# A two-block transformer kernel: softmax off GpSimd, convolutions ahead of the state-space heads, decay rows spread by transfers

## The chip, the cores and the metric

The kernel runs on one core of one Trainium2 chip. The metric is the device time of the whole program in microseconds; lower is better. The program takes 512 tokens of 1024 numbers in float32 through two blocks, once.

## The reference, cut to what matters

The first block is a mixer layer (windowed means, a sparse attention over selected keys), a cross attention to 256 memory tokens and a SwiGLU layer. The second block is two hybrid layers, and each of them runs a sliding-window attention and a state-space ("SSD") scan on the same input:

```python
def hybrid_layer(x, ...):
    q, k, v, z_attn, z_ssm, xbc, dt_raw = split(x @ w_in)
    attn = sliding_window_attention(q, k, v, sinks) * silu(z_attn)
    xbc = silu(causal_depthwise_conv(xbc, conv_w, conv_b))      # 12 x 128 channels
    xs, bm, cm = split(xbc)                                     # 8 + 2 + 2
    y = ssd_chunked(xs, softplus(dt_raw + dt_bias), -exp(a_log), bm, cm) + xs * d_skip
    ssm = gated_rmsnorm(y, z_ssm, ssm_norm_w)                   # y * silu(z), two groups
    return layer_norm(ALPHA * x + concat(attn, ssm) @ w_out, ln_g, ln_b)

def ssd_chunked(xs, dt, a, bm, cm):                             # 4 chunks of 128, 16 heads of 64
    a_cs = cumsum(dt * a) in each chunk
    y_diag[l] = sum_s (cm[l] . bm[s]) * exp(a_cs[l] - a_cs[s]) * xdt[s]    # s <= l
    y_off[l]  = (cm[l] . state before the chunk) * exp(a_cs[l])
    return y_diag + y_off
```

## The kernel before, in words

All activations stand with 128 channels on the partitions and 512 tokens along the row. Each float32 operand of a matmul is split into a rounded part and a rest (`hi`, `lo`), and a product is three matmuls: `hi*hi` and `hi*lo` (L147, L148), then `lo*hi` (L152). A projection of 1024 channels onto 128 is 24 matmuls (`proj`, `mm3`). `weights()` brings one such 128x1024 piece: SP issues the load of `wraw` (L104), ScalarE casts it to `whi` (L107), VectorE subtracts for `wlo` (L108); each has three buffers. `split` and `pair` do the same to activations (L129, L130, or L132, L133 with a scale).

A hybrid layer (`hybrid`) goes in this order: the first four gates z and dt; the convolutions of B, C and of channels 0 to 4 (`conv`: a projection, L905 on ScalarE, three passes on VectorE, a tanh); then a loop of eight head pairs. Each turn holds one more projection (channels 5 to 7, then the last four gates), `decay(j+1)` for the next pair and `heads(j)` for this one. Then the two keys (L132, L133 and copies of each half to the other half of the partitions, L1114 on GpSimd), the token values (96 matmuls, L1127 to L1129), and the attention loop over 16 heads (`scores`, `transposed`, `values`) with its own projections of queries and gates.

`decay(j)` makes, for both heads of a pair, the 128x512 factors `exp(-(relu(a_s - a_l))) * cb`. A matmul with a column of `sel` spreads a head's row of `a_cs` over the partitions in PSUM (L1041), ScalarE takes the difference and relu in four pieces (L1045), exponentials of the row (L1047) and of the whole (L1048), and GpSimd or VectorE multiplies by `cb` (L1049). `heads(j)` has 16 matmuls L1061 and 6 of L1067, and VectorE adds up (L1069 to L1071); L1098 is the gate, and L1078 the norm's scaling. The softmax of the attention is normalised at L1169, half on GpSimd and half on VectorE, ahead of the transposes L1183; L1154 and L1155 are the scores. The memory attention does the same at L763.

The feed-forward stage keeps `x` in DRAM (`xd`): 16 writes at L788 and 16 reads at L868, on ScalarE's queue.

SP's instructions stand in program order. On the other engines a scheduler sets the order when the program is built; each engine then goes through its list strictly in order, and a row whose input is late holds all rows behind it.

## Time and profile before

| | |
|---|---|
| median of 3 runs | 1673.09 us (1672.94 to 1673.29) |
| the profiled execution | 1672.5 us, span 1670.7 us |
| mean granted TensorE clock | 0.993 |
| TensorE matmul busy | 1621.6 us (97%) |
| VectorE, ScalarE, GpSimd busy | 1115.1 us (67%), 838.0 us (50%), 239.2 us (14%) |
| DMA | 166.50 MB, 100 GB/s over the span |
| the two hybrid layers | about 834 to 1657 us of the span |

The profile is of one execution. The engines' rows give busy time; the chain follows the end of the program back to what released each step; the waits list what ended each idle time of an engine. Where TensorE is idle, nothing else makes up for it unless the chain shows otherwise.

### The profile page before, as it was taken

What the parts mean: (1) busy time and instruction counts of PE and PEld (TensorE: products, weight loads), DVE (VectorE), ACT (ScalarE), POOL (GpSimd) and SP (SyncE); (2) the same over time, 40 slices, a digit from 0 to 9 for tenths busy, and PEclk for the clock granted to TensorE, in tenths of its full rate; (3) what the DMA queues carried; (4) which work ended last, traced back from release to release, by engine and by line L of the source; (5) the groups of instructions that cost most, each with busy time, mean ns of one, the idle gap of its engine ahead of it and who ended that gap; (6) DMA issues with size and microseconds to landing.
All of it is one profiled execution on the core that took longest, in us unless ns stands there. A gap on an engine that the chain in (4) does not pass through costs nothing.

```text
span 1670.7 us, 24187 instructions
## 1 busy us (share of the span) xinstructions
PE 1621.6 (97%) x9046; PEld 1362.4 (82%) x9046; DVE 1115.1 (67%) x2199; ACT 838.0 (50%) x1648; POOL 239.2 (14%) x267
## 2 busy tenths in 40 slices
PE   8999999999999999999999999999999999999996
PEld 5778888889888888889988677777998867777786
DVE  6779866548885545523677888765487788866447
ACT  4443255336763233223554776664355477766424
POOL 2010113010200000000000223221230023222121
PEclk9999999999999999999999999999999999999998
DMA  6522322143143233234632122111452211212133
GB/s 223 196 96 76 119 96 76 64 151 119 62 150 104 89 101 101 87 102 129 212 93 89 38 64 89 64 64 56 141 177 82 79 38 57 96 61 65 66 103 112
DMA packets 57719, 166.50 MB, mean 100 GB/s; under 512 B 6673, under 2 KB 15841, under 8 KB 57601
## 3 DMA queue, kind: packets, MB, share of 16 engines
q1 hardware_dynamic: 49216, 155.21, 29.0%
q10 hardware_dynamic: 8384, 9.73, 1.8%
q8 instruction: 71, 1.16, 0.3%
q14 instruction: 48, 0.39, 0.1%
HBM read 158.61 MB, written 8.93 MB: 100 GB/s over the span
## 4 chain that ended last, share of the span: by engine, by line
PE 78%; DVE 11%; ACT 5%; issue 2%; POOL 2%; DMA 1%; SPq 0%; ACTq 0%; DVEq 0%; POOLq 0%
PE psmm L148 21%; PE psmm L152 21%; PE psmm L147 21%; DVE wlo L108 2%; POOL w L1169 2%; PE psmm L175 2%; PE psmm L173 2%; PE psmm L174 2%; ACT w L1164 1%; DVE w L1160 1%; DVE G L130 1%; PE pstr L1061 1%; PE pstr L1183 1%; PE pslg L561 1%; PE pslg L1020 1%
## 5 line engine op out<-in xcount | busy, mean ns | idle before, releaser
L147 PE MATMUL psmm<-G,whi 128*128 128x512 f32 (+1 forms) x1196 | 468.5, 393 | 1.3 <-ACT whi L107 1.3
L148 PE MATMUL psmm<-G,whi 128*128 128x512 f32 (+1 forms) x1196 | 464.3, 389 | 0.0
L108 DVE TENSOR_TENSOR wlo<-wraw,whi 128x1024 fp32r<-128x1024 f32 (+3 forms) x265 | 320.4, 1210 | 184.8 <-ACT whi L107 99.2
L107 ACT CAST whi<-wraw 128x1024 fp32r<-128x1024 f32 (+3 forms) x265 | 270.9, 1025 | 340.3 <-PE psmm L148 291.3
L152 PE MATMUL psmm<-G,wlo 128*128 128x512 f32 (+1 forms) x1196 | 296.3, 388 | 0.0
L148 PEld LDWEIGHTS psmm<-G,whi 128*128 128x128 f32 x1196 | 225.3, 188 | 47.2 <-issue 4.2
L147 PEld LDWEIGHTS psmm<-G,whi 128*128 128x128 f32 x1196 | 225.3, 188 | 47.2 <-issue 2.4
L152 PEld LDWEIGHTS psmm<-G,wlo 128*128 128x128 f32 x1196 | 222.7, 189 | 46.4 <-issue 1.5
L148 PE MATMUL psmm<-R,whi 128*128 128x256 f32 (+1 forms) x732 | 222.7, 326 | 0.0
L147 PE MATMUL psmm<-R,whi 128*128 128x256 f32 (+1 forms) x732 | 222.6, 326 | 0.0
L147 PEld LDWEIGHTS psmm<-R,whi 128*128 128x128 f32 x732 | 139.2, 190 | 11.8 <-issue 0.3
L148 PEld LDWEIGHTS psmm<-R,whi 128*128 128x128 f32 x732 | 139.2, 190 | 11.5
L152 PE MATMUL psmm<-R,wlo 128*128 128x256 f32 (+1 forms) x732 | 138.1, 326 | 0.0
L152 PEld LDWEIGHTS psmm<-R,wlo 128*128 128x128 f32 x732 | 112.8, 190 | 11.5
L198 POOL TENSOR_TENSOR acc<-acc,sq 128x512 f32<-128x512 f32 (+1 forms) x42 | 53.4, 1272 | 454.4 <-ACT sq L197 454.4
L1164 ACT ACTIVATE w<-w,st 128x256 f32<-128x256 f32 (+1 forms) x128 | 60.2, 471 | 33.5 <-DVE st L1162 33.2
L1169 POOL TENSOR_SCALAR w<-w,st 128x256 f32<-128x256 f32 x64 | 46.1, 730 | 134.6 <-DVE st L1167 127.0
L209 ACT ACTIVATE sq<-ht 128x512 f32<-128x512 f32 (+1 forms) x48 | 29.4, 613 | 58.5 <-DVE ht L907 29.3
L1049 POOL TENSOR_TENSOR R<-R,R 128x512 f32<-128x512 f32 x16 | 21.7, 1353 | 228.3 <-ACT R L1048 228.3
L907 DVE SCALAR_TENSOR_TENSOR ht<-psmm,cwh,ht 128x511 f32<-128x511 f32 (+2 forms) x72 | 53.5, 743 | 1.2
L837 DVE TENSOR_TENSOR sq<-psmm,G 128x512 f32<-128x512 f32 (+1 forms) x24 | 15.5, 645 | 57.3 <-PE psmm L152 57.3
L566 POOL TENSOR_TENSOR G<-G,G 128x384 f32<-128x384 f32 (+2 forms) x24 | 28.9, 1217 | 162.1 <-DMA G<-ts 93.4
(348 smaller groups left out, 2701.8 us busy)
## 6 DMA issues: line engine op xcount, KB each, us to landing
wraw<-w_in SPq DMA_DIRECT2D x112, 512.0 KB, 3.4
wraw<-w_out SPq DMA_DIRECT2D x56, 512.0 KB, 3.8
wraw<-w_down SPq DMA_DIRECT2D x24, 512.0 KB, 3.5
wraw<-w_gate SPq DMA_DIRECT2D x22, 512.0 KB, 3.3
wraw<-w_up SPq DMA_DIRECT2D x22, 512.0 KB, 3.3
wraw<-w_down SPq DMA_DIRECT2D x12, 384.0 KB, 3.2
wraw<-w_proj_attn SPq DMA_DIRECT2D x8, 512.0 KB, 3.4
ts<-t SPq DMA_DIRECT2D x4, 640.0 KB, 7.0
```

What stands on the lines that cost most here:

```text
L107: nc.scalar.copy(hi[:, :n], raw[:, :n])
L108: nc.vector.tensor_tensor(lo[:, :n], raw[:, :n], hi[:, :n].bitcast(F32), ALU.subtract)
L147: nc.tensor.matmul(out, whi[:, c], xh, start=start and k == 0, stop=False)
L148: nc.tensor.matmul(out, whi[:, c], xl, start=False, stop=False)
L152: nc.tensor.matmul(out, wlo[:, c], xh, start=False, stop=stop and k == n - 1)
L173: nc.tensor.matmul(o, whi[:, cc], xh[:, c], start=k == 0 and i % 2 == 0, stop=False, skip_group_check=True)
L174: nc.tensor.matmul(o, whi[:, cc], xl[:, c], start=False, stop=False, skip_group_check=True)
L175: nc.tensor.matmul(o, wlo[:, cc], xh[:, c], start=False, stop=k == n - 1, skip_group_check=True)
L198: (eng or nc.gpsimd).tensor_tensor(acc, acc, t, ALU.add)
L907: nc.vector.scalar_tensor_tensor(y[:, s:], pt[:, : S - s], cw(3 - s), y[:, s:], ALU.mult, ALU.add)
L1164: nc.scalar.activation(prs[b], prs[b], AF.Exp, bias=nm[:, b : b + 1], accum_out=sm[:, b : b + 1])
L1169: (nc.gpsimd if b % 2 else nc.vector).tensor_scalar(prs[b], prs[b], rc[:, b : b + 1], 1.0, ALU.mult, ALU.mult)
```

## The change

It does seven things. Weights' rests are cut in pieces of 512 columns inside the attention loop only. The memory softmax and the attention softmax are normalised on VectorE alone. The 32 `xd` transfers go from ScalarE's queue to SP's. The last three `w_o_mem` pieces are held in buffers of their own, and three feed-forward weights are loaded ahead. The rows `a_cs` and their exponentials are written to DRAM once per layer, and four SP transfers per head pair spread them over the partitions, two pairs ahead; the 16 matmuls per layer of L1041 and the exponentials of L1047 go, half of the relu passes go to VectorE (L1057) and the product with `cb` is all VectorE's (L1059). Convolutions 5 and 6 come before the heads; the loop's turns then hold convolution 7, four gates, the token values and the two keys. The keys' half copies, eight per layer, are SP transfers (L1101).

```diff
--- before.py
+++ after.py
@@ -75,6 +75,7 @@
...
+        self.piece = 2 * S
...
@@ -105,7 +106,9 @@
         hi = self.wp.tile([P, 1024], F32R, tag="whi", bufs=3, name=self.nm("whi"))
         lo = self.wp.tile([P, 1024], F32R, tag="wlo", bufs=3, name=self.nm("wlo"))
         nc.scalar.copy(hi[:, :n], raw[:, :n])
-        nc.vector.tensor_tensor(lo[:, :n], raw[:, :n], hi[:, :n].bitcast(F32), ALU.subtract)
+        for o in range(0, n, self.piece):
+            c = slice(o, min(o + self.piece, n))
+            nc.vector.tensor_tensor(lo[:, c], raw[:, c], hi[:, c].bitcast(F32), ALU.subtract)
         return hi, lo
 
     def held(self, src, tag, n=1024):
@@ -760,7 +763,7 @@
                 nc.scalar.activation(p, bank[:, 256 * i : 256 * i + 256], AF.Exp, bias=nm[:, i : i + 1], scale=r[:, i : i + 1], accum_out=sm[:, i : i + 1])
             nc.vector.reciprocal(rc, sm)
             for i, p in enumerate(parts):
-                (nc.vector if i else nc.gpsimd).tensor_scalar(p, p, rc[:, i : i + 1], 1.0, ALU.mult, ALU.mult)
+                nc.vector.tensor_scalar(p, p, rc[:, i : i + 1], 1.0, ALU.mult, ALU.mult)
             return parts
 
         def values(hd, c, prs):
@@ -785,7 +788,7 @@
 
         def each(k, c, x):
             scale(k, c, x)
-            nc.scalar.dma_start(self.xd[k][:, c], x)
+            nc.sync.dma_start(self.xd[k][:, c], x)
 
         def out(j, c):
             o = self.ps()[:, :256]
@@ -800,13 +803,12 @@
             nc.sync.dma_start(kv[i].bitcast(F32), self.spill[i])
         wo = [self.held(a["w_o_mem"][0], "G")]
         queries(B, lambda k: values(k // 2, A, pa[k // 2]) if k % 2 else None)
-        wo += [self.weights(a["w_o_mem"][1]), self.weights(a["w_o_mem"][2])]
+        wo += [self.held(a["w_o_mem"][j], "R") for j in (1, 2, 3)]
         for j in range(8):
-            if j == 4:
-                wo.append(self.weights(a["w_o_mem"][3]))
             out(j, A)
             if j < 4:
                 pb.append(logits(j, B))
+        self.ahead = [self.weights(z) for z in (a["w_gate"][0], a["w_up"][0], a["w_gate"][1])]
         for j in range(4):
             values(j, B, pb[j])
             if j == 0:
@@ -842,8 +844,7 @@
         full = slice(0, S)
         hid += self.pairs("R", 2)
         g = [self.f("ht") for _ in range(2)]
-        first = [self.weights(z) for z in (a["w_gate"][0], a["w_up"][0], a["w_gate"][1])]
-        first.append(self.held(a["w_up"][1], "R"))
+        first = self.ahead + [self.held(a["w_up"][1], "R")]
         for c in self.HALVES:
             for i, pt in enumerate(self.units_by_k(first, h, c)):
                 (up if i % 2 else gate)(i // 2, c, g[i // 2][:, c], pt)
@@ -865,7 +866,7 @@
 
         def src(k, c):
             t = self.s("w256", (P, 256), 9)
-            nc.scalar.dma_start(t, self.xd[k][:, c])
+            nc.sync.dma_start(t, self.xd[k][:, c])
             return t
 
         self.h = self.pairs("G")
@@ -880,9 +881,6 @@
         self.dist = self.load("dist", [P, 256], nc.sync)
         self.sinks = self.load("sinks", [P, 32], nc.sync)
         self.small = self.load("small16", [16, 4], nc.sync)
-        sel = self.load("sel", [48, 16], nc.sync)
-        self.sel = self.cp.tile([48, 16], F32R, tag="selr", name="selr")
-        nc.vector.tensor_copy(self.sel, sel)
 
     def hybrid(self, L):
         nc, a = self.nc, self.a
@@ -952,9 +950,10 @@
         nc.vector.tensor_scalar(av, av, -1.0, None, ALU.mult)
         nc.vector.tensor_scalar(e, dtf, av, None, ALU.mult)
         nc.vector.tensor_tensor_scan(acs, seg, e, 0.0, ALU.mult, ALU.add)
-        ahl = self.s("ahl", (48, S), dt=F32R)
-        nc.vector.memset(ahl.bitcast(F32), 0.0)
-        self.split(acs, ahl[0:16, :], ahl[32:48, :])
+        self.acsd = self.dp.tile([2, 16, S], F32, tag=f"acs{L}", name=f"acs{L}")
+        nc.scalar.dma_start(self.acsd[0], acs)
+        nc.scalar.activation(seg, acs, AF.Exp)
+        nc.scalar.dma_start(self.acsd[1], seg)
         B, C = BC[:2], BC[2:]
 
         ptd = self.ps("tr")
@@ -1030,24 +1029,34 @@
             xs.append(conv(j, "G"))
         xs.append(conv(4, "G"))
         tokens(0)
+        for j in range(5, 7):
+            xs.append(conv(j, "G"))
+
+        def decay_rows(j):
+
+            dfs, ee = [self.f("R") for _ in range(2)], self.f("R")
+            for e_, df in enumerate(dfs):
+                row = self.acsd[:, 2 * j + e_, :]
+                nc.sync.dma_start(df, row[:1].broadcast_to([P, S]))
+                nc.sync.dma_start(ee[64 * e_ : 64 * e_ + 64, P:], row[1:, P:].broadcast_to([64, S - P]))
+            return dfs, ee
 
         def decay(j):
 
-            ee = self.f("R")
-            dfs = []
-            for e_ in range(2):
+            dfs, ee = rows.pop(0)
+            if j < 6:
+                rows.append(decay_rows(j + 2))
+            for e_, df in enumerate(dfs):
                 hd = 2 * j + e_
-                pb = self.ps("lg")
-                nc.tensor.matmul(pb, self.sel[:, hd : hd + 1].broadcast_to([48, P]), ahl, start=True, stop=True)
-                df = self.f("R")
                 for c in range(4):
                     cc = slice(c * P, (c + 1) * P)
-                    nc.scalar.activation(df[:, cc], pb[:, cc], AF.Relu, bias=atok[:, c * 16 + hd : c * 16 + hd + 1], scale=-1.0)
-                rows = slice(64 * e_, 64 * e_ + 64)
-                nc.scalar.activation(ee[rows, P:], pb[rows, P:], AF.Exp)
-                nc.scalar.activation(df, df, AF.Exp, scale=-1.0)
-                (nc.vector if e_ else nc.gpsimd).tensor_tensor(df, df, cb[hd // 8], ALU.mult)
-                dfs.append(df)
+                    at = atok[:, c * 16 + hd : c * 16 + hd + 1]
+                    if e_:
+                        nc.scalar.activation(df[:, cc], df[:, cc], AF.Relu, bias=at, scale=-1.0)
+                    else:
+                        nc.vector.tensor_scalar(df[:, cc], df[:, cc], at, 0.0, ALU.subtract, ALU.min)
+                nc.scalar.activation(df, df, AF.Exp, scale=-1.0 if e_ else 1.0)
+                nc.vector.tensor_tensor(df, df, cb[hd // 8], ALU.mult)
             return dfs, ee
 
         def heads(j, ws, ee):
@@ -1079,16 +1088,54 @@
                 cat[8 + i] = self.pair(t, "R")
 
 
+
+        top, bot = slice(0, 64), slice(64, P)
+        kt = []
+
+        def keys(j):
+            pt = self.proj(W[j], h)
+            ks = [[self.r("G") for _ in range(2)] for _ in range(2)]
+            for (kh, kl), r, o in zip(ks, (top, bot), (bot, top)):
+                self.split(pt[r], kh[r], kl[r], 0.125)
+                for t in (kh, kl):
+                    nc.sync.dma_start(t[o].bitcast(F32), t[r].bitcast(F32))
+            return ks
+
+        def token_values():
+            vs = [self.f("G") for _ in range(2)]
+            pv = [self.ps("mm") for _ in range(2)]
...
+            for v, pt in zip(vs, pv):
+                nc.scalar.copy(v, pt)
+            return vs
+
+
         cat = [None] * 16
         accs = []
+        rows = [decay_rows(0), decay_rows(1)]
         ws = decay(0)
         for j in range(8):
             g = j // 4
-            if j < 3:
-                xs.append(conv(5 + j, "G"))
-            elif j < 7:
+            if j == 0:
+                xs.append(conv(7, "G"))
+            elif j < 5:
                 zs.append(self.f("R"))
-                silu(zs[-1], self.proj(W[25 + j], h))
+                silu(zs[-1], self.proj(W[27 + j], h))
+            elif j == 5:
+                vs = token_values()
+            else:
+                kt.append(keys(j - 6))
             nxt = decay(j + 1) if j < 7 else None
             if j == 3:
                 tokens(1)
@@ -1101,35 +1148,6 @@
             if j % 4 == 0:
                 accs.append(self.f("acc"))
             self.sumsq(y, accs[-1], j % 4 == 0)
-
-
-        top, bot = slice(0, 64), slice(64, P)
-        kt = []
-        for j in range(2):
-            pt = self.proj(W[j], h)
-            ks = [[self.r("G") for _ in range(2)] for _ in range(2)]
-            for (kh, kl), r, o in zip(ks, (top, bot), (bot, top)):
-                self.split(pt[r], kh[r], kl[r], 0.125)
-                for t in (kh, kl):
-                    nc.gpsimd.tensor_copy(t[o], t[r].bitcast(F32))
-            kt.append(ks)
...
         gated_norm(1, accs[1])
 
         def scores(t, q):
@@ -1166,7 +1184,7 @@
             nc.vector.tensor_tensor(sm, sm, es, ALU.add)
             nc.vector.reciprocal(rc, sm)
             for b in range(4):
-                (nc.gpsimd if b % 2 else nc.vector).tensor_scalar(prs[b], prs[b], rc[:, b : b + 1], 1.0, ALU.mult, ALU.mult)
+                nc.vector.tensor_scalar(prs[b], prs[b], rc[:, b : b + 1], 1.0, ALU.mult, ALU.mult)
             return prs
 
         def transposed(prs):
@@ -1207,6 +1225,7 @@
             return qs
 
 
+        self.piece = S
         q = queries(0)
         gate, pts = {}, {}
         prs = None
@@ -1231,6 +1250,7 @@
                 cat[i] = self.pair(gate[i], "R", 0.5)
             prs = nxt
 
+        self.piece = 2 * S
         order = list(range(8, 16)) + list(range(8))
         acc, acc2, rs = self.f("acc"), self.f("acc"), self.f("rs")
         vs = [self.f("G") for _ in range(KD)]
```

The lists that the scheduler makes of it move. In each layer the new lines have these numbers: L147, L148, L152 are L150, L151, L155; L107, L108 are L108, L111; L905 is L903; L132, L133 are L135, L136; L1048 is L1058, L1045 is L1055; L1061, L1067 are L1070, L1076; L1078 is L1087; L1098 is L1145; L1169 is L1187; L204 is L207.

SP's list at the end of the first hybrid layer's heads, before the change (loads of the two keys' weights, of the token values' two, and of queries 0 and 1):

```order
L104 DMA wraw_1761_9253<-w_in2 128x1024
L104 DMA wraw_1769_9296<-w_in2 128x1024
L104 DMA wraw_1781_9343<-w_in2 128x1024
L104 DMA wraw_1784_9397<-w_in2 128x1024
L104 DMA wraw_1802_9487<-w_in2 128x1024
L104 DMA wraw_1816_9557<-w_in2 128x1024
```

and with the change (two loads for the token values, key 0's, its four half copies, key 1's, its four, and queries 0; the `G` numbers 9303 to 9306 are the split parts of key 0):

```order
L105 DMA wraw_1730_9130<-w_in2 128x1024
L105 DMA wraw_1733_9184<-w_in2 128x1024
L105 DMA wraw_1739_9272<-w_in2 128x1024
L1101 DMA G_1743_9303<-G_1743_9303 64x512
L1101 DMA G_1744_9304<-G_1744_9304 64x512
L1101 DMA G_1745_9305<-G_1745_9305 64x512
L1101 DMA G_1746_9306<-G_1746_9306 64x512
L105 DMA wraw_1765_9382<-w_in2 128x1024
L1101 DMA G_1769_9413<-G_1769_9413 64x512
L1101 DMA G_1770_9414<-G_1770_9414 64x512
L1101 DMA G_1771_9415<-G_1771_9415 64x512
L1101 DMA G_1772_9416<-G_1772_9416 64x512
```

The load of key 1's weights now stands behind copies of key 0's parts, and the load of the first queries' weights behind those of key 1's.

ScalarE's list where the loop of heads begins, before the change (two casts, for convolution 7 and for the gate after it; the L905 are convolutions 4 and 5, the last row is the first of `decay`):

```order
L107 CAST whi_8774<-wraw_8772 128x1024
L905 ACTIVATE ht_8500<-psmm_8508,cwh_7787 128x512
L209 ACTIVATE sq_8537<-ht_8500 128x512
L107 CAST whi_8854<-wraw_8852 128x1024
L1023 COPY R_8551<-pslg_8549 128x512
L905 ACTIVATE ht_8609<-psmm_8617,cwh_7787 128x512
L1045 ACTIVATE R_8591<-pslg_8589,dtt_8302 128x128 x4
```

and with the change, from the moment that convolution 6 has left TensorE (`psmm_8644`) to the cast for convolution 7 (`whi_8713`):

```order
L903 ACTIVATE ht_8636<-psmm_8644,cwh_7795 128x512
L1058 ACTIVATE R_8676<-R_8676 128x512
L1055 ACTIVATE R_8677<-R_8677,dtt_8310 128x128
L1055 ACTIVATE R_8684<-R_8684,dtt_8310 128x128
L1058 ACTIVATE R_8677<-R_8677 128x512
L1055 ACTIVATE R_8684<-R_8684,dtt_8310 128x128 x3
L1058 ACTIVATE R_8684<-R_8684 128x512
L1055 ACTIVATE R_8691<-R_8691,dtt_8310 128x128
L212 ACTIVATE sq_8673<-ht_8636 128x512
L1058 ACTIVATE R_8683<-R_8683 128x512
L1055 ACTIVATE R_8691<-R_8691,dtt_8310 128x128 x3
L108 CAST whi_8713<-wraw_8711 128x1024
```

The casts of weights stood ahead of the decay work, and now the one for convolution 7 stands behind a pass that waits for convolution 6 and behind decay work of three pairs.

ScalarE's list between the fourth gate's product (`psmm_9061`) and the cast for the token values (`whi_9132`), with the change; `rs` is the first group's norm:

```order
L212 ACTIVATE R_9054<-psmm_9061 128x512
L229 ACT_TABLE_LOAD
L229 ACTIVATE rs_9344<-pstr_9345,eps_85 128x512
L1058 ACT_TABLE_LOAD
L1058 ACTIVATE R_9088<-R_9088 128x512
L1055 ACTIVATE R_9089<-R_9089,dtt_8310 128x128 x4
L108 CAST whi_9132<-wraw_9130 128x1024
```

Between these TensorE's list holds only the rest of pair 6's products, the norm's sum L207 and three products of pair 7. Before, projections stood between the pairs, and the token values behind key 1.

## Rows read from the trace of the kernel before

**Rows 1.** The page's busy line, and TensorE's clock in 40 slices.

```profile
PE 1621.6 (97%) x9046; PEld 1362.4 (82%) x9046; DVE 1115.1 (67%) x2199; ACT 838.0 (50%) x1648; POOL 239.2 (14%) x267
...
PEclk9999999999999999999999999999999999999998
```

**Rows 2.** The page's chain that ended last, by engine.

```profile
PE 78%; DVE 11%; ACT 5%; issue 2%; POOL 2%; DMA 1%; SPq 0%; ACTq 0%; DVEq 0%; POOLq 0%
```

**Rows 3.** Waits of TensorE: line waited for: us in total, times, longest.

```profile
PE pstr L1183 <- POOL w L1169: 5.7, 14, 0.6
PE pslg L1154 <- DVE G L130: 5.0, 2, 2.5
PE pstr L204 <- DVE acc L198: 4.4, 2, 3.4
PE pstr L1061 <- POOL R L1049: 2.1, 2, 1.3
```

**Rows 4.** Windows round two stalls: length, busy by engine, granted clock, DMA share.

```profile
460.00:475.00 15.00, 11.24 (x63) 10.20 (x62) 12.24 (x24) 10.72 (x24) 0.37 (x1) 0.77 0.43 139
...
1022.00:1030.00 8.00, 5.48 (x22) 4.20 (x21) 7.88 (x16) 4.32 (x7) 0.00 (x0) 0.79 0.21 67
```

**Rows 5.** Timeline of TensorE in a head pair: start, us, instruction.

```profile
975.47 0.72 PE L1041 MATMUL pslg<-ahl,selr 48*128 48x512 f32 x2
...
976.12 0.44 PE L1061 MATMUL pstr<-R,G 128*64 128x128 f32 x4
```

**Rows 6.** Timeline of the attention, 1088 to 1091 us.

```profile
1088.44 2.04 POOL L1169 TENSOR_SCALAR w<-w,st 128x256 f32<-128x256 f32 x2 [5.34 <-DVE st L1167]
...
1090.53 0.44 PE L1183 MATMUL pstr<-ident,w 128*128 128x128 f32 x2 [0.40 <-POOL w L1169]
```

**Rows 7.** VectorE's scaling passes of line 453, alone: duration ns min/median/max, forms.

```profile
L453 DVE TENSOR_SCALAR G<-G,st x32: 278/380/486, 219.7 to 295.5; 128x384 f32<-128x384 f32 x8, 128x128 f32<-128x128 f32 x8, 128x256 f32<-128x256 f32 x8, 128x512 f32<-128x512 f32 x8
```

**Rows 8.** Groups by form, ScalarE and VectorE: us busy, mean ns, idle before.

```profile
L107 ACT CAST whi<-wraw 128x1024 fp32r<-128x1024 f32 x243 | 254.6, 1050 | 283.5 <-PE psmm L148 248.1 <-PE psmm L174 14.0 <-issue 9.3
...
L1169 DVE TENSOR_SCALAR w<-w,st 128x256 f32<-128x256 f32 x32 | 18.5, 578 | 0.0
...
L1048 ACT ACTIVATE R<-R 128x512 f32<-128x512 f32 x32 | 20.2, 632 | 0.4
...
L905 ACT ACTIVATE ht<-psmm,cwh 128x512 f32<-128x512 f32 x24 | 18.6, 776 | 5.6 <-PE psmm L152 3.9 <-PE pslg L1020 1.5
...
L209 ACT ACT_TABLE_LOAD x9 | 11.5, 1283 | 1.3 <-DVE ht L907 0.9 <-DVE ht L829 0.3
```

**Rows 9.** Timeline of ScalarE in the loop of heads, 976 to 980 us.

```profile
976.98 0.60 ACT L209 ACTIVATE R<-psmm 128x512 f32<-128x512 f32 x1
977.47 1.14 ACT L1045 ACTIVATE R<-pslg,dtt 128x128 f32<-128x128 f32 x4
```

**Rows 10.** Timeline of a head pair's products on TensorE, 968 to 970 us.

```profile
968.55 1.09 PE L1061 MATMUL pstr<-R,G 128*64 128x128 f32 x16
...
969.57 0.94 PE L1067 MATMUL pstr<-R,R 128*128 128x128 f32 x6
```

**Rows 11.** Timeline, a key's split and the norm's scaling, 995 to 1022 us.

```profile
998.19 0.57 ACT L132 ACTIVATE G<-psmm 64x512 fp32r<-64x512 f32 x1
...
1001.14 0.68 DVE L133 SCALAR_TENSOR_TENSOR G<-psmm,G 64x512 fp32r<-64x512 f32 x1
...
1021.15 1.41 DVE L1078 SCALAR_TENSOR_TENSOR ht<-G,vecs,rs 128x512 f32<-128x512 f32 x2
```

**Rows 12.** DMA issues: count, KB each, median us to landing.

```profile
wraw<-w_in SPq DMA_DIRECT2D x112, 512.0 KB, 3.4
...
ts<-t SPq DMA_DIRECT2D x4, 640.0 KB, 7.0
...
G<-ts ACTq DMA_DIRECT2D x8, 256.0 KB, 2.7
```

**Rows 13.** Waits of SP's own queue.

```profile
SPq L115 <- DMA xd<-G: 20.2, 1, 20.2
```

More of the change, by code (lines that the diff above doesn't have):

```diff
@@ L1349, in _constants @@
     c["segs"] = seg
-    sel = np.zeros((48, 16), np.float32)
-    for h in range(16):
-        for r in (h, 32 + h):
-            sel[r, h] = 1.0
-    c["sel"] = sel
     return c
```

28 lines of the change are left out of this document (12 added, 16 removed).

## The prediction

> **What bounds the kernel now.** I read the page first: TensorE is busy 97% of the span, at full clock in nearly all of the 40 slices [rows 1], and the chain that ended last is 78% TensorE [rows 2]. So time is gained where TensorE's own work goes or where one of its few waits goes, and lost wherever its next operand comes late. Then I read its waits [rows 3]: the sum that matters is small, some 17 us, the largest for the half of the attention's normalisation that runs on GpSimd. Third, windows round the two longest of them, 3.4 and 2.5 us [rows 3]: the mean granted clock is 0.77 over 15 us and 0.79 over 8 us there [rows 4], so behind the stall TensorE ran some time at the lower of its two levels. What that takes is 0.23 x 15 = 3.4 us and 0.21 x 8 = 1.7 us, beside the stall itself. The sum below stands against the profiled 1672.5 us, which is 0.6 us under the median of 1673.09.
>
> **What the change takes away.** *Decay products.* The pair of L1041 matmuls starts at 975.47 and the next matmul at 976.12 [rows 5], so one costs 0.33 us of TensorE's time; 32 of them are 10.4 us (by their summed busy time, which counts pipelining twice, 13.2).
>
> *Stalls in and behind the heads.* The waits for GpSimd's product with `cb` (2.1 us) and for the split of a query ahead of the first scores (5.0 us) stand in [rows 3]. In the new order neither is last. With two half-clock spells of 1.7 us behind the 5.0 [rows 4] they give 10.5 us back, 11 with smaller waits of 0.2 to 0.5 us; the new waits at the same places are counted below.
>
> *Attention normalisation.* Fourteen times TensorE waits for GpSimd at L1183 [rows 3]: GpSimd's two pieces take 2.04 us beside VectorE's subtraction, and the last two transposes wait [rows 6]. Scaling passes of VectorE took 0.28 to 0.49 us in the mixer [rows 7], where GpSimd does no part of them, and 0.58 for this form here, beside GpSimd's part [rows 8]; four pieces are 0.28 + 3 x 0.38 = 1.4 us, or 2.0 by the slower row. By the first they are done when the transposes want them, by the second they are as late as now. GpSimd falls still, so I take the first: 5.7 us of waits and 0.1 us of refilling at each, 7 us; the ends are 0 and 9.4 (0.25 of refilling).
>
> *Memory to feed-forward.* Nine matmuls of the feed-forward stage now stand ahead of the norm's sum L204, whose longest wait is 3.4 us [rows 3]; they cover 1.1 us of it and shorten the spell. I take 2 us, ends 0 and 5.
>
> *At nothing:* the `xd` transfers on SP's queue (they are 128 KB and the weights behind them are loaded several ahead), the key copies themselves (wanted only by the scores, after the first queries), and the row spreads, which are issued two pairs ahead, some 15 us; the nearest rows are 2.7 us for 256 KB and 7.0 for 640 KB [rows 12]. Their cover is that lead; without it a pair would wait up to 7 us, which is the third rival. Half of the relu passes and all products with `cb` on VectorE cost TensorE nothing by themselves: VectorE is 67% busy [rows 1]. All gains: 10.4 + 11 + 7 + 2 = **30.4 us**.
>
> **What the change puts in.** Each list is strictly in order, so I add up what stands between TensorE's last product and its next operand. Prices: a cast 1.05, an exponential 0.63, a convolution's first pass 0.78, a table load 1.28 [rows 8], four relu pieces 1.14 and a pass like a tanh or a logarithm 0.60 [rows 9], a pair's products 1.09 and 0.94 [rows 10], a key's split 0.57 on ScalarE and 0.68 on VectorE, one scaling 0.70 [rows 11], a weight load 3.4 [rows 12].
>
> (a) *Convolution 7.* Its cast stands behind the pass that waits for convolution 6, four exponentials, nine relu pieces and a tanh: 0.78 + 4 x 0.63 + 9 x 0.285 + 0.60 + 1.05 = 7.5 us. TensorE has 12 head products meanwhile, 1.1 us: a stall of 6.4.
>
> (b) *The second and fourth gates.* The second gate's cast stands behind the square of a head pair's output, for which VectorE must first have that pair's products and gate: 3.4. After the third gate pair 6's products wait for states that VectorE makes one after another: 4.0. Both are sums of three to five passes of 0.6 to 0.7 us; either could be 2.
>
> (c) *Token values.* From the fourth gate's product: tanh 0.60, table 1.28, logarithm 0.60, table 1.28, exponential 0.63, relu 1.14, cast 1.05 = 6.6, and TensorE has 1.6 us of products: 5.0.
>
> (d) *Key 1.* SP cannot issue the load of its weights before key 0 is split: 0.57 + 2 x 0.68 on two engines, and a head pass of 0.7 between them, is 2.6; the issue of the last copy and of the load 0.3 each, the load 3.4, the cast 1.05: 7.7 us. Seven head products and a norm's sum cover 1.0: 6.7.
>
> (e) *Queries 0.* The same behind key 1, but its splits stand on VectorE in the second group's norm. Counted from the cast of key 1: table, logarithm, table and two passes on ScalarE 4.5; two passes and two scalings on VectorE 2.8; two rests 1.4; then split, two scalings, split 2.8: 11.5. Issue, load and cast make it 16.3, less the 5.45 us of key 1's 24 matmuls: 10.9. It is at least 7 if the norm's part is done earlier.
>
> Together 6.4 + 3.4 + 4.0 + 5.0 + 6.7 + 10.9 = 36.4 us a layer, **73 us** in two. The ends: if each wait overlaps the earlier parts of the next, 5.5 + 2 + 2 + 4 + 5.5 + 7 = 26 a layer; if VectorE is late everywhere by one weight subtraction, some 7 more. To this come the half-clock spells: four of the six stalls in a layer are at least as long as the two of [rows 4], so eight times 1.7, **13.6 us** (ends 0, if the clock stays up, and 27, if all are the longer kind).
>
> Sum: 1672.5 - 30.4 + 73 + 13.6 = **1729 us**.
>
> **A rule against this.** What the trace shows: SP's queue stood 20.2 us behind one transfer that had to wait for a write of `xd` [rows 13]; what waits at the head of SP's list holds the loads behind it, and (d) and (e) rest on that. The Trainium skill, page "DMA: Bandwidth & Descriptors", section "Rules for kernel authors", says that transfers issued from SP, ScalarE or GpSimd all run on the same 16 engines and that spreading them over issuers only saves issue time; taken by itself it would make sixteen copies on SP's queue cost their issue alone, some 5 us off the path, and the time that of the second rival. The trace's row does not contradict the shared engines, but it shows a cost that the rule leaves out.
>
> **The rivals.** *One: the casts and loads run ahead (faster).* If the first 1.5 pairs of decay work were done before convolution 6 ends, as ScalarE's 50% busy share would allow [rows 1], and the loads came back early enough, the new stalls would mostly not arise and the gains would stand alone: 1672.5 - 30.4 = 1642 us. The point from which it decides is 15 us of new stalls a layer. Against it: the cast of convolution 7 stands behind a pass that reads convolution 6's product, in the list, and no earlier work frees it. Chance 0.06.
>
> *Two: SP's queue costs only its issue.* Then (d) and (e) go, 17.6 us a layer, and four spells: 1729 - 35.2 - 6.8 = 1687 us. For it: only key 0's split parts are copied, and a load might be issued earlier; against it, the order of SP's list and [rows 13]. Chance 0.14.
>
> *Three: the row spreads are late.* The spread of one row over 128 partitions has no row in the trace; its 256 KB take at least the 2.7 us of [rows 12], and at worst four times 7.0 us for a pair against a lead of 15. Then five or six pairs a layer wait 3 us or so, and more of the clock falls: 1729 + 30 = 1760 us and up. For it: the transfers share SP's queue with weights; against it, DMA moves 100 GB/s in the mean, and 223 at most in a slice of the page. Chance 0.17.
>
> *Four: the change does less than it says*, because the old projections were no filler and neither gains nor stalls are large: within 1670 to 1676. Against it is the removal of 10 us of products, which is certain. Chance 0.03.
>
> **How the numbers follow.** The forecast has 0.60. A difference of 0.2%, 3.3 us, is about what a measurement of this kernel can tell from no change. Faster: the first rival, 0.06, and a little of the fourth, 0.07; same 0.03; slower 0.90. The range's lower end takes the low bound of the stalls (52 + 13.6 - 30.4 gives 1708) and most of the second rival down to 1688; the upper end takes VectorE's lateness and the longer spells (1729 + 14 + 13 = 1756) and the nearer half of the third: 1688 to 1764.
>
> **What would show it.** In the profile after: TensorE's busy time about 1611 us at full clock (10 less), its waits led by `whi` L108 and by weights' loads, two stalls of 6 to 11 us behind each layer's keys with SP's queue waiting for VectorE L136, a stall of 6 us ahead of convolution 7, half-clock slices near the end of each layer's heads, and no wait of L1201 for GpSimd. The forecast is wrong if TensorE's wait for `whi` is under 10 us a layer, if a key's load lands before the other key's product has ended, or if the waits are instead on the decay rows' transfers.

## The result, and the profile after

The changed kernel took 1726.12 us (median of 4 runs, 1724.29 to 1727.55) against 1673.01 before: a ratio of 1.0317, 95% interval 1.030 to 1.0335. It is slower by 53.1 us; 1729 us was forecast. The profiled execution took 1727.55 us, its span is 1725.8.

The page's busy line and TensorE's clock, beside [rows 1]:

```profile
PE 1631.9 (95%) x9014; PEld 1374.5 (80%) x9014; DVE 1134.5 (66%) x2381; ACT 809.1 (47%) x1555; POOL 151.8 (9%) x163
...
PEclk9999999999999999999999988999999998899998
```

TensorE has 32 matmuls fewer and is busy 10 us longer, where the prediction had 10 us less: some of its work ran at the lower clock level, in these slices at the end of each layer's heads, and in shorter spells that the slices do not show (0.77 over the 6 us from 935). Its waits, beside [rows 3] (us in total, times, longest):

```profile
PE psmm L150 <- ACT whi L108: 25.8, 8, 9.9
PE pstr L1070 <- DVE R L1059: 13.7, 6, 4.3
PE pstr L207 <- POOL acc L201: 10.3, 2, 5.1
...
PE pstr L207 <- DVE acc L201: 2.9, 2, 1.7
PE pstr L1070 <- DVE G L1078: 2.9, 4, 1.5
PE psmm L780 <- ACT ht L132: 2.3, 2, 2.1
...
PE pstr L1201 <- DVE w L1187: 0.8, 4, 0.2
```

The waits for GpSimd ahead of the attention's transposes and for its product with `cb` are gone; the late casts, the decay factors L1059 and the second norm's sum have come. One layer's stretch from the first matmul of dt to the first score, before (first line) and after (window's ends and length, busy time of PE, PEld, DVE, ACT, POOL, clock):

```profile
860.10:1025.10 165.00, 161.24 (x854) 125.13 (x852) 133.79 (x182) 107.50 (x200) 29.93 (x24) 1.00 0.24 74
```

```profile
863.70:1056.50 192.80, 164.88 (x833) 129.97 (x831) 141.38 (x228) 94.64 (x154) 9.11 (x8) 0.92 0.33 99
```

So 27.8 us of the loss lie here, and 28.1 in the second layer's like stretch. The attention's stretch, from the first score to the last product with the values, was 129.2 and 128.8 us and is 126.8 in both layers; what stands ahead of the first layer's dt is 3.6 us longer in this execution. These add up to the 55.1 us by which the span grew, within 0.2.

The end of the keys, by the chain that ended last (start, us, what):

```profile
1021.92 0.60 ACT G L135
1022.54 0.68 DVE G L136
1023.22 0.65 DVE G L1078
1023.90 0.70 DVE G L136
1024.66 0.46 SPq L1101
1025.21 4.13 DMA wraw<-w_in
1029.37 1.04 ACT whi L108
...
1041.24 0.70 DVE G L136
1041.96 0.46 SPq L1101
1042.48 4.01 DMA wraw<-w_in
1046.51 1.05 ACT whi L108
1047.61 0.79 PE psmm L150
```

This is the chain that the prediction added up: split, copies, load, cast, twice. No compute engine's list of waits has one for a spread decay row; the rows landed in 5.0 us in the median:

```profile
R<-acs SPq DMA_DIRECT2D x32, 256.0 KB, 5.0
```

### The profile page after: what moved, and what is told of

It is laid out like the page before. It is cut to its first block, busy times and chain, and to the rows that moved or that the text cites. A ratio compares the mean times of both kernels' runs of the same rounds, so it can differ in the third digit from the quotient of the medians.

```text
span 1725.8 us, 24143 instructions
## 1 busy us (share of the span) xinstructions
PE 1631.9 (95%) x9014; PEld 1374.5 (80%) x9014; DVE 1134.5 (66%) x2381; ACT 809.1 (47%) x1555; POOL 151.8 (9%) x163
## 4 chain that ended last, share of the span: by engine, by line
PE 82%; DVE 10%; ACT 4%; issue 2%; DMA 2%; POOL 0%; SPq 0%; DVEq 0%; ACTq 0%; POOLq 0%
PE psmm L150 22%; PE psmm L151 22%; PE psmm L155 21%; PE pstr L1201 1%; PE psmm L1216 1%; PE psmm L178 1%; PE psmm L176 1%; PE psmm L177 1%; DMA wraw<-w_in 1%; PE psmm L687 1%; ACT w L1182 1%; PE pslg L564 1%; PE pslg L1172 1%; DVE wlo L111 1%; PE pstr L1070 1%
## 5 line engine op out<-in xcount | busy, mean ns | idle before, releaser
L150 PE MATMUL psmm<-G,whi 128*128 128x512 f32 (+1 forms) x1196 | 473.4, 397 | 25.8 <-ACT whi L108 25.8
L151 PE MATMUL psmm<-G,whi 128*128 128x512 f32 (+1 forms) x1196 | 467.6, 392 | 0.0
L111 DVE TENSOR_TENSOR wlo<-wraw,whi 128x1024 fp32r<-128x1024 f32 (+3 forms) x294 | 320.5, 1094 | 190.7 <-ACT whi L108 96.0
L108 ACT CAST whi<-wraw 128x1024 fp32r<-128x1024 f32 (+3 forms) x262 | 267.4, 1023 | 353.2 <-PE psmm L151 295.8
L155 PE MATMUL psmm<-G,wlo 128*128 128x512 f32 (+1 forms) x1196 | 293.0, 386 | 0.0
L150 PEld LDWEIGHTS psmm<-G,whi 128*128 128x128 f32 x1196 | 228.7, 191 | 78.1 <-ACT whi L108 30.6
L151 PEld LDWEIGHTS psmm<-G,whi 128*128 128x128 f32 x1196 | 228.8, 191 | 45.5 <-issue 0.8
L155 PEld LDWEIGHTS psmm<-G,wlo 128*128 128x128 f32 x1196 | 222.3, 188 | 45.0
L151 PE MATMUL psmm<-R,whi 128*128 128x256 f32 (+1 forms) x684 | 210.6, 329 | 0.0
L150 PE MATMUL psmm<-R,whi 128*128 128x256 f32 (+1 forms) x684 | 210.5, 329 | 0.0
L150 PEld LDWEIGHTS psmm<-R,whi 128*128 128x128 f32 x684 | 130.0, 190 | 11.8 <-issue 0.3
L151 PEld LDWEIGHTS psmm<-R,whi 128*128 128x128 f32 x684 | 130.0, 190 | 11.5
L155 PE MATMUL psmm<-R,wlo 128*128 128x256 f32 (+1 forms) x684 | 130.4, 329 | 0.0
L155 PEld LDWEIGHTS psmm<-R,wlo 128*128 128x128 f32 x684 | 106.2, 190 | 11.5
L905 DVE SCALAR_TENSOR_TENSOR ht<-psmm,cwh,ht 128x511 f32<-128x511 f32 (+2 forms) x72 | 53.6, 744 | 6.9 <-ACT ht L903 5.7
L200 ACT ACTIVATE sq<-G 128x256 f32<-128x256 f32 (+1 forms) x76 | 35.0, 463 | 43.6 <-DVE G L1145 19.5
L1178 DVE CUSTOM_DVE_ANT_0 w<-pslg,w,sinks 128x256 f32<-128x256 f32 (+1 forms) x128 | 51.2, 446 | 0.3
L1160 POOL TENSOR_SCALAR w<-dist 128x256 f32<-128x256 f32 x32 | 22.5, 702 | 323.0 <-PE pstr L1201 266.3
```

Source lines behind the costliest of these rows:

```text
L108: nc.scalar.copy(hi[:, :n], raw[:, :n])
L111: nc.vector.tensor_tensor(lo[:, c], raw[:, c], hi[:, c].bitcast(F32), ALU.subtract)
L150: nc.tensor.matmul(out, whi[:, c], xh, start=start and k == 0, stop=False)
L151: nc.tensor.matmul(out, whi[:, c], xl, start=False, stop=False)
L155: nc.tensor.matmul(out, wlo[:, c], xh, start=False, stop=stop and k == n - 1)
L200: self.last_sq = nc.scalar.activation(t, src, AF.Square)
```

## The experiments

Each ratio is to runs of the kernel before that were timed beside that kernel, on the same chip; the medians of the kernel before were 1672.1 to 1673.4. The table has the stretch of the first layer from dt to the first score, from each profile.

| kernel | median us | ratio, 95% interval | stretch us |
|---|---|---|---|
| before | 1673.0 | 1 | 165.0 |
| the change | 1726.12 | 1.0317, 1.030 to 1.0335 | 192.8 |
| e1 loads ahead of the copies | 1700.42 | 1.0162, 1.0148 to 1.0176 | 180.0 |
| e6 as e1, norm behind the loop | 1693.02 | 1.013, 1.0115 to 1.0146 | 179.1 |
| e3 keys behind the loop | 1696.49 | 1.0137, 1.0121 to 1.0152 | 177.5 |
| e4 whole loop as before | 1692.92 | 1.012, 1.0106 to 1.0134 | 175.2 |
| e5 decay rows by products | 1686.24 | 1.0085, 1.0071 to 1.0099 | 173.7 |
| d3 rows one pair ahead | 1724.87 | 1.0313, 1.0299 to 1.0327 | 192.3 |
| d4 decay passes shared as before | 1735.70 | 1.0379, 1.0363 to 1.0395 | 197.8 |
| b2 softmax alone | 1670.71 | 0.9988, 0.9979 to 0.9997 | 164.8 |
| b3 feed-forward parts alone | 1673.11 | 1.0009, 1.000 to 1.0018 | 165.0 |
| b6 softmax, norm behind the loop | 1662.73 | 0.9944, 0.9932 to 0.9957 | 160.9 |
| c1 b6 and the change's loop | 1668.19 | 0.9973, 0.9962 to 0.9984 | 163.6 |
| c2 as c1, SP copies, loads ahead | 1666.71 | 0.9967, 0.9955 to 0.998 | 164.4 |

**e1: do the loads behind the copies cost it?**

```diff
         def keys(j):
-            pt = self.proj(W[j], h)
+            pt = self.proj(None, h, w=kw.pop(0))
+            kw.append(self.weights(W[16 * j + 1 - j]))
```

> The changed kernel with one thing different: the weights of key 1 and of queries 0 are loaded ahead of the half copies in SP's list, the copies stay SP transfers. Theory (the loads stand behind copies that wait for a key's split; 7.3 and 10.0 us of TensorE's idle time a layer hang on that): most of the 17 us a layer goes, 3 to 6 us of it return as a wait for the second norm's sum and for the key copies ahead of the first scores, and with half-clock time the kernel takes 1694 to 1706 us. Rival (the norm of the second head group, not the loads, sets the end of the keys): 1718 to 1726 us.

1700.42 us: the theory, 25.7 us less than the change by taking two loads per layer from behind the copies. (The lengths of single waits below are the idle times of the timeline. The expectations here and for e3 and e6 have some of them longer: 7.3, 10.0 and 4.6 for what the timeline has as 5.5, 9.8 and 4.3.) Its waits (the L150 row was 25.8):

```profile
PE pstr L1070 <- DVE R L1059: 13.7, 6, 4.3
PE psmm L150 <- ACT whi L108: 9.2, 6, 2.1
```

The decay factors' row has not moved. TensorE's list has moved with the loads: the second norm's sum L207, ahead of key 1 in the change, now stands in the middle of key 1's product.

**e3: keys and token values behind the loop, copies on GpSimd.**

```diff
-            elif j == 5:
-                vs = token_values()
-            else:
-                kt.append(keys(j - 6))
...
+        kt = [keys(0), keys(1)]
+        vs = token_values()
         gated_norm(1, accs[1])
```

> The changed kernel with the keys and the token values behind the loop of heads and the keys' copies on GpSimd, as before; convolutions 5 and 6 stay ahead of the heads. Theory (SP's queue and the missing filler behind the heads): the two waits of 7.3 and 10.0 us a layer become one of about 3 ahead of the first scores, as in the kernel before, and the time is 1688 to 1698 us. The wait of 4.6 us between the fourth gate and pair 7 stays, and so do those ahead of convolution 7. Rival (the order of the loop matters most, not its end): 1710 us and up.

1696.49 us, inside the theory's range. The waits at the keys became the old one ahead of the first score, 2.6 us; the 4.3 us ahead of pair 7 stayed, as did those round convolution 7.

**e4: the whole loop as before, decay rows still by transfers** (as e3, and convolutions 5 to 7 and the gates in their old turns).

> The changed kernel with the whole loop of heads, the keys and the token values as before, so that only the spread of the decay rows by transfers, the softmax and the feed-forward parts of the change are left. Theory (the reordering alone costs, the decay rows' transfers are hidden and give 10 us of products back): 1662 to 1674 us. Rival (the transfers or the passes moved to VectorE hold the heads up): 1685 us and up, with TensorE's waits on the decay rows.

1692.92 us: the theory fell. With every reordering undone the kernel still lost 20 us, where 10 less had been the reckoning. The waits of e4:

```profile
PE pslg L1019 <- DVE ht L1017: 18.0, 8, 5.0
PE pstr L1068 <- DVE R L1057: 6.5, 3, 3.0
```

The first is new: the state sums L1019, in the first layer 5.7 us of it in the first channel group and 3.1 in the second. In e4's list the eight transposes ahead of them and the products of pairs 0 and 1 follow at once, and the three convolutions that used to stand between them come after both pairs. The place in the lists makes this wait, not data that come late: the first state input of VectorE is ready at much the same time before (first row) and in e4 (second row), but before TensorE had the 24 matmuls of a convolution to do until then. In e4 the last weights' load ahead of the pairs was issued at 900.40 and landed within 6.6 us, yet the next cast is at 941.20, in ScalarE's list behind a decay pass for which ScalarE idled 6 us:

```profile
922.07 0.68 DVE L1018 TENSOR_TENSOR ht<-pstr,dend 128x512 f32<-128x512 f32 x1
...
922.65 0.68 DVE L1017 TENSOR_TENSOR ht<-pstr,dend 128x512 f32<-128x512 f32 x1
...
923.38 3.78 PE L1019 MATMUL pslg<-ht,G 128*128 128x512 f32 x4 [5.00 <-DVE ht L1017]
...
932.13 0.63 ACT L1056 ACTIVATE R<-R 128x512 f32<-128x512 f32 x1 [6.05 <-DVE R L1055]
...
941.20 1.03 ACT L108 CAST whi<-wraw 128x1024 fp32r<-128x1024 f32 x1
```

So spreading the rows by transfers does something besides taking 16 matmuls out.

**e5: the change, with products in place of the transfers.**

```diff
-                nc.sync.dma_start(df, row[:1].broadcast_to([P, S]))
...
+                nc.tensor.matmul(pb, self.sel[:, hd : hd + 1].broadcast_to([48, P]), ahl, start=True, stop=True)
...
-                nc.vector.tensor_tensor(df, df, cb[hd // 8], ALU.mult)
+                (nc.vector if e_ else nc.gpsimd).tensor_tensor(df, df, cb[hd // 8], ALU.mult)
```

> The changed kernel with the decay rows spread by products again (16 a layer, with the exponentials on ScalarE and the product with cb shared with GpSimd, as before); all the reordering and SP's half copies stay. Theory (the products were also what kept projections between the head pairs: without them the scheduler sets pairs next to each other, and TensorE waits for the decay passes and the states): the 10.4 us of products come back, and 8 to 12 us of waits a layer in the heads go, with their half-clock time: 1705 to 1720 us. Rival (convolutions 5 and 6 ahead of the heads make those waits, whatever spreads the rows): 1730 to 1740 us.

1686.24 us, further than the theory's range: 39.9 us less than the change, though TensorE has its 32 matmuls back (and the passes their old engines, which d4 below shows to be no help). In e5's list a projection of 24 matmuls stands between each two of the first four pairs; in the change's list pairs 1 and 2, and 3 and 4, follow each other with none between. What e5 still waits for is SP's list:

```profile
PE psmm L150 <- ACT whi L108: 14.6, 5, 8.5
```

**d3 and d4: the lead of the rows, and who does the passes.**

```diff
-        rows = [decay_rows(0), decay_rows(1)]
+        rows = [decay_rows(0)]
...
-            if j < 6:
-                rows.append(decay_rows(j + 2))
+            if j < 7:
+                rows.append(decay_rows(j + 1))
```

> The changed kernel with the decay rows spread one pair ahead in place of two. Theory (rows that are there early let the decay passes of two pairs stand ahead of the weights' casts in ScalarE's list, and pairs stand next to each other in TensorE's): with one pair less ahead the waits round convolution 7 and the gates shrink by 3 to 8 us a layer, 1705 to 1720 us. Rival (the lead does not matter, the waits come with the missing products alone): 1722 to 1730 us; if the rows' transfers themselves are late with the shorter lead, more.

1724.87 us: the rival. One pair less of lead changes nothing, so it is not the second pair of early rows that bunches the work.

```diff
-                    if e_:
-                        nc.scalar.activation(df[:, cc], df[:, cc], AF.Relu, bias=at, scale=-1.0)
-                    else:
-                        nc.vector.tensor_scalar(df[:, cc], df[:, cc], at, 0.0, ALU.subtract, ALU.min)
+                    nc.scalar.activation(df[:, cc], df[:, cc], AF.Relu, bias=at, scale=-1.0)
...
-                nc.vector.tensor_tensor(df, df, cb[hd // 8], ALU.mult)
+                (nc.vector if e_ else nc.gpsimd).tensor_tensor(df, df, cb[hd // 8], ALU.mult)
```

> The changed kernel with the decay passes shared as before: all relu pieces on ScalarE, the product with cb half on GpSimd; the rows still come by transfers. Theory (where the passes stand in the lists costs, not which engine does them): 1722 to 1736 us. Rival (the passes moved to VectorE, which also does the convolutions' sums, hold the heads): 1700 to 1715 us.

1735.70 us, in the theory's range, though the engine does matter, the other way: the passes on VectorE were no loss, and back on ScalarE and GpSimd they cost 9.6 us more.

**e6: the norm of the first group behind the loop** (e1, and the call of `gated_norm(0, ...)` moved from turn 6 to just ahead of `gated_norm(1, ...)`).

> The kernel e1 (loads ahead of the copies) with the norm of the first head group moved behind the loop, next to the second one's. Theory (the 4.6 us between the fourth gate and pair 7 are ScalarE's two table loads and the logarithm of this norm, which stand ahead of pair 7's exponentials): they go in both layers, 1687 to 1694 us. Rival (both norms together now hold the first scores, and the wait only moves): 1697 to 1703 us.

1693.02 us, 7.4 under e1, in the theory's range; but its trace is less clean than the number. The wait of 4.3 us ahead of pair 7 became one of 3.3 us and one of 1.2 us, both for decay factors; the second layer's stretch fell from 178.7 to 176.6 us and the first's only from 180.0 to 179.1. The rest is 1.1 and 1.5 us in the two attention stretches and 1.9 us ahead of the first layer, where the two kernels are alike. So the norm holds pair 7 only in part, and the theory is borne out by the time more than by the place.

e6 also answers a rival that nothing above speaks of: the row spreads stand in SP's list too, and where they wait for a buffer they hold the loads behind them, as the half copies do. In the change SP waits 17.6 us in all for such buffers, and the casts wait 17.8 us for loads. In e6 SP waits nearly as long for them, and yet the casts hardly wait for a load, so these spreads are not what makes the casts late:

```profile
SPq L1040 <- PE pstr L1070: 16.6, 4, 8.4
...
ACT whi L108 <- DMA wraw<-w_in: 1.8, 1, 1.8
```

**b2, b3, b6: parts alone, on the kernel before.**

```diff
-                (nc.gpsimd if b % 2 else nc.vector).tensor_scalar(prs[b], prs[b], rc[:, b : b + 1], 1.0, ALU.mult, ALU.mult)
+                nc.vector.tensor_scalar(prs[b], prs[b], rc[:, b : b + 1], 1.0, ALU.mult, ALU.mult)
```

> The kernel before with both softmaxes normalised on VectorE alone and the weights' rests in two pieces inside the attention. Theory: the 14 waits for GpSimd go, 4 to 7 us less, 1666 to 1669 us. Rival (VectorE becomes as late as GpSimd was): 1672 to 1675 us.

1670.71 us: 2.6 less, between theory and rival. The attention's stretch is 127.1 us in both layers, about 2 less than before.

> The kernel before with the feed-forward parts alone: xd transfers on SP's queue, three w_o_mem pieces held and split, three feed-forward weights loaded ahead. Theory (the splits of the held pieces stand on ScalarE and VectorE ahead of the memory softmax, and cost there what the shorter wait ahead of the feed-forward stage gives, and some more): 1674 to 1678 us. Rival (as predicted, 2 us gained): 1670 to 1672 us.

1673.11 against 1672.09, between the theory's range and the rival's: no gain, and at most 3 us of loss. Its waits show both sides, L204 shorter than in [rows 3], and new ones in the memory attention:

```profile
PE pstr L204 <- DVE acc L198: 2.7, 2, 1.5
...
PE psmm L777 <- ACT ht L129: 2.1, 1, 2.1
PE psmm L778 <- DVE sq L130: 1.7, 3, 1.2
```

b6 is b2 with the memory softmax left alone and this:

```diff
-            if j == 6:
-                gated_norm(0, accs[0])
...
+        gated_norm(0, accs[0])
         gated_norm(1, accs[1])
```

> The kernel before with the attention softmax normalised on VectorE alone, the weights' rests in two pieces there, and the first group's norm behind the loop. The memory softmax stays as before. Theory: 3 to 4 us less from the attention and 1 to 3 us from the norm's table loads leaving the loop, 1665 to 1669 us. Rival (two norms ahead of the first scores lengthen the wait of 2.7 us there): 1671 to 1675 us.

1662.73 us, faster than both kernels, and better than its theory: not only the table loads left the loop, the wait of 2.5 us ahead of the first score went too [rows 3], in both layers, and with it the lower clock behind it (1.00 over both stretches). The stretch from dt to the first score, 164.8 and 165.1 us in b2, is 160.9 and 160.8. Its longest wait behind the start of the program is none of the heads or the scores, but the one ahead of the feed-forward stage:

```profile
PE pstr L207 <- DVE acc L201: 4.4, 2, 3.4
```

**c1, c2: the change's loop on b6, with products.** Convolutions 5 and 6 ahead of the heads, the token values and the keys as turns of the loop; c1 copies on GpSimd, c2 by SP with the two loads ahead, as in e1.

> The kernel b6 with the change's loop: convolutions 5 and 6 ahead of the heads, token values and keys as turns of the loop, half copies on GpSimd, decay rows by products. Theory (with the products in the lists this loop keeps a projection between pairs and costs nothing): within 4 us of b6's 1662.7. Rival (the loop itself costs, by late casts ahead of the keys): 1668 to 1680 us.

> As c1, but with the half copies as SP transfers and the weights of key 1 and queries 0 loaded ahead of them. Theory (SP's copies cost only where a load stands behind them): as c1 or a little less, 1657 to 1666 us. Rival (a copy that lands late holds the first scores): over 1668 us.

1668.19 and 1666.71 us. c1 is 5.5 over b6, 1.5 more than its theory allowed and at the lower end of the rival's; c2 is 0.7 above its theory's range and under its rival's. Each taken against the kernel before that was timed beside it, c1 is 4.9 and c2 3.4 us over b6. So the new loop costs 3 to 5 us where the products are in the lists and the norm behind it, and SP's copies are harmless with the loads ahead of them. c2's own new wait is in the attention's first heads:

```profile
PE pslg L1169 <- DVE st L1175: 8.1, 4, 2.3
```

## Why the prediction was right, point by point

*The sum came out by errors that cancelled.* 56 us were forecast over the profiled execution and 55.1 found. The stretch of heads and keys was to lose 32.6 us a layer net (36.5 of new waits and 6.8 of lower clock, less 5.2 of products and 5.5 of old waits) and lost 27.8 and 28.1. The attention was to give 7 and gave 4.3, the stages ahead of the first layer to give 2, and they lost 3.6 in this execution. So the nearness of the total, less than 3 us off in the median, is in part luck. Wait by wait, in idle time of TensorE in the first layer (second layer):

| | forecast | found |
|---|---|---|
| (a) convolution 7 | 6.4 | 3.4 (3.8) |
| (b) second and fourth gates | 7.4 | 4.8 (4.8) |
| (c) token values | 5.0 | 4.3 (4.3) |
| (d) key 1 | 6.7 | 5.5 (5.3) |
| (e) queries 0 | 10.9 | 9.8 (9.9) |
| together | 36.4 | 27.8 (28.1) |

*(a) Convolution 7.* 7.5 us were added up from the end of convolution 6 to the end of the cast, and the trace has the cast end at 942.74 and the first matmul at 943.14, against an end of convolution 6 at 935.56:

```profile
934.27 1.29 PE L155 MATMUL psmm<-G,wlo 128*128 128x512 f32 x5
937.91 0.40 PE L1070 MATMUL pstr<-R,G 128*64 128x128 f32 x2 [2.34 <-DVE R L1059]
938.24 1.63 PE L1076 MATMUL pstr<-R,R 128*128 128x128 f32 x6
939.80 1.97 PE L1070 MATMUL pstr<-R,G 128*64 128x128 f32 x14
941.71 1.03 ACT L108 CAST whi<-wraw 128x1024 fp32r<-128x1024 f32 x1
...
942.78 0.43 PE L1070 MATMUL pstr<-R,G 128*64 128x128 f32 x2 [1.01 <-DVE G L1078]
943.14 0.51 PE L150 MATMUL psmm<-G,whi 128*128 128x512 f32 x1
```

The length was right and the booking wrong: TensorE waited for pair 0's factors and for the sum of pair 0 before the cast could hold it, and of the 6.4 us that were forecast as a stall 3.4 were idle. The rest went into 24 head products, not 12, at the lower clock level (six of L1076 take 1.63 us here and 0.94 in [rows 10]).

*(b) Second and fourth gates.* 7.4 us a layer were forecast. The gaps there are 0.2, 0.4 and 1.4 up to the second gate, 1.0 behind it, and 1.2, 0.4 and 0.2 between the third gate and the fourth: 4.8 in all, 2.6 less and near the low ends that the prediction gave. The largest of each:

```profile
961.55 0.50 PE L150 MATMUL psmm<-G,whi 128*128 128x512 f32 x1 [1.43 <-ACT whi L108]
...
982.40 1.13 PE L1019 MATMUL pslg<-ht,G 128*128 128x512 f32 x2 [1.16 <-ACT R L1022]
```

*(c) Token values.* 5.0 forecast, 4.3 found, by the steps that were named up to the exponential: the fourth gate's tanh, table load, logarithm, table load, exponential. But what TensorE waits for is the factors of pair 7, whose products its list has ahead of the token values, and not the cast of the token values' weights:

```profile
996.02 1.28 ACT L229 ACT_TABLE_LOAD   x1
997.53 0.69 ACT L229 ACTIVATE rs<-pstr,eps 128x512 f32<-128x512 f32 x1 [0.23 <-DVE acc L220]
998.24 1.28 ACT L1058 ACT_TABLE_LOAD   x1
999.53 0.63 ACT L1058 ACTIVATE R<-R 128x512 f32<-128x512 f32 x1
...
1001.03 0.66 PE L1070 MATMUL pstr<-R,G 128*64 128x128 f32 x2 [4.26 <-DVE R L1059]
```

*(d), (e) Keys.* 6.7 and 10.9 forecast, 5.5 and 9.8 found, and e1 shows the cause of the two together: with the loads ahead of the copies 25.7 us go. For (e) TensorE's list has nothing between key 1 and the queries, and the load alone holds it. For (d) two waits end almost together: TensorE first waits at L207, which stands ahead of key 1 in its list, for GpSimd's norm sum, and 1.3 us after that sum the load lands (1029.34).

```profile
1028.03 2.07 PE L207 MATMUL pstr<-acc,ones 128*128 128x512 f32 x2 [5.13 <-POOL acc L201]
...
1030.47 0.80 PE L150 MATMUL psmm<-G,whi 128*128 128x512 f32 x1 [0.36 <-ACT whi L108]
```

In that order key 1 would have started only 0.4 us sooner with its weights at hand. That e1 gains at (d) too rests on both, the load and the new place of L207, and the two were not tried apart.

*Lower clock.* 6.8 us a layer forecast, as an estimate from two spells. The first layer's stretch without the idle 27.9 us is 164.9; before it was 161.2, of which 5.2 went: 8.9 us of stretching, a little more. It is also why TensorE's busy time rose where the prediction looked for about 1611 us. (The two waits of [rows 3] that it calls the longest are so only behind the start of the program: TensorE's first matmul, at L684, waits 5.4 us, which the change does not touch.)

*Decay products.* 10.4 us were booked as a gain with no other effect, and that is the step that misled, though not the sum: (a) to (c) were charged to the reordering of the loop, and e4, e5, c1 and c2 say otherwise. With products the change's loop costs 3 to 5 us (c1, c2); with transfers every loop tried, old or new, loses some 20 us or more (e4, e6). c2 and e6 differ by 26.3 us, and by the spread of the rows with the engines of its passes, the memory softmax and the feed-forward parts. d4 shows that the passes' engines are no loss, b2 that the softmax is none, and b3 allows at most 3 us for the last. What is shown is that the waits come with the transfers, in whatever loop, that no compute engine waits for the transfers themselves, and that neither their lead (d3) nor the engines of the passes (d4) make them. That the scheduler, with no product in TensorE's list to hold a pair back, puts pairs side by side and the projections elsewhere is what its lists show, and e4's rows show what that costs: the same state input at the same time, and no projection to fill the 5 us ahead of it. Why the scheduler does so is argued and not shown; an order written by hand with the rows by transfers, which would settle it, was not tried. So of the 27.8 us of idle time a layer, the 15.3 at the keys came in the main by the mechanism that was forecast; the 12.4 of (a) to (c) came at the places that were forecast and, together, at two thirds of the length, by a cause that the prediction had put at nothing.

*Attention.* The waits for GpSimd went as forecast (5.7 us), and VectorE's 128x256 form took 0.35 us, the price of [rows 7] and not that of [rows 8]:

```profile
L1187 DVE TENSOR_SCALAR w<-w,st 128x256 f32<-128x256 f32 x96 | 27.9, 348 | 0.0
...
L1145 DVE TENSOR_TENSOR G<-G,R 128x512 f32<-128x512 f32 x16 | 11.0, 685 | 0.1
```

The two stretches gave 4.3 of the 7 us. The prediction took the refilling behind each wait as the rest; that it was overrated fits, but no run takes it apart.

*Memory to feed-forward.* 2 us were forecast, and the stretch ahead of the first layer's dt ended at 863.7 us in place of 860.1. That is mostly the execution: the eight profiles with the change's parts there (the change, e1, e3 to e6, d3, d4) have 860.3 to 863.7, 862.1 in the middle, and those without (before, b6, c1, c2) 860.1 to 861.9; b3's profile, of one of its two longest executions, has 864.5. So it is nothing or a loss of about 1 us, as b3 says, and no gain of 2. The shorter wait is there, but three splits of held weights were not costed: they put waits of the memory attention's products on ScalarE and VectorE (L780 above, and b3).

*The rivals.* The first (casts run ahead) and the third (late rows) are refuted by the waits; the second, that SP's queue costs only its issue, by e1: what stands behind a transfer that waits for an engine cost 25.7 us. The Trainium skill's rule on issuers ("DMA: Bandwidth & Descriptors", "Rules for kernel authors"), that spreading transfers over issuers only saves issue time, is not contradicted for the transfers themselves: c2 with SP's copies and the loads ahead is no slower than c1 without.

## What to carry to other kernels

Read a queue as a list: a transfer that waits for a result holds every load behind it, so put the loads that come next ahead of it. Where a scheduler sets the order, a removed instruction is not only its own time; look at what its place kept apart in the new list before booking the gain. And a late reduction with table loads belongs behind the loop: moving one call was worth some 7 us between b2 and b6 (which also leaves the memory softmax on GpSimd), more than the normalisation on VectorE.

## What was not expected of the hardware

VectorE's gate pass of 128x512 with two operands took 1.12 us in the mean before, with GpSimd at work in the loop, and 0.69 with GpSimd out of it (L1098 before, L1145 after). Before, 7 of its 16 instances ran beside a GpSimd instruction and took 1.57 to 1.80 us, and the other 9 took 0.68 to 0.69. The Trainium skill, page "SBUF — State Buffer", section "SBUF: two separate sides", says that the two share one port pair as an exclusive lock, for a VectorE instruction with two SBUF inputs against a GpSimd one that reads SBUF, and these times agree with it. A spread of one DRAM row over 128 partitions, 256 KB, landed in 5.0 us; other transfers of 256 KB in the same profile have medians of 2.5 to 6.0, so it is among the slower ones and no exception.
